# Which tokens open the first pass of a hybrid attention layer

## The chip, the cores and the metric

The kernel runs on one core of one Trainium2 chip. The metric is device time in microseconds (us). The median of three runs before the change is 1921.53 us (1916.76 to 1921.9).

## The reference

One decoder step of a layer that has two groups of heads, for 2048 prompt tokens and for a sample group of 8 x 8 tokens. All data are float32.

```python
xn = rmsnorm(h, g_mix_norm)                      # h: tokens x 1024
z = xn @ w_in
q_c, kv_c, gate_mla, q_g, k_g, v_g, a_g, gate_gla = split(z)   # 256, 160, 512, 256, 256, 512, 16, 512
q = rmsnorm(q_c) @ w_qup                         # 8 heads, 64 + 32 rotary
c_kv, k_rope = rmsnorm(kv_c[:128]), rope(kv_c[128:])
o_mla = attention(q, c_kv, k_rope) * silu(gate_mla)
log_a = log_sigmoid(a_g @ w_gla_a2 + b) / 16
o_gla = rmsnorm(gated_linear_attention(q_g, k_g, v_g, log_a)) * silu(gate_gla)
h = h + concat(o_mla, o_gla) @ w_out
h = h + sigmoid(h @ w_ple_gate) * (p @ w_ple_proj)
y = rmsnorm(h, g_final)
```

Prompt tokens attend causally among themselves; the sample's tokens attend to 4096 cached positions through a page table and to the new ones. The outputs are y, the latents c_kv, the rotary keys and the states of the linear attention, for both groups.

## The kernel before, in words

The program has five stages, of which the change touches the first. Pass A makes, from the first 944 columns of `w_in`, the latents, queries, keys, values, the gates of the attention and the log decays. Pass B is the gated linear attention. Then come the decode attention of the sample interleaved with the prompt's attention, and the output products.

A product of float32 matrices is carried by three float32r passes: each operand is split into hi and lo, and hi x hi, hi x lo and lo x hi are summed in one PSUM bank. `mm3` (L63, L64, L65) does that for 128 or more stationary columns, `mm2` (L71, L72, L74) for the 64 tokens of the sample, where hi and lo stand side by side. A split costs one ScalarE (ACT) or GpSimd (POOL) pass for hi and one VectorE (DVE) pass for lo: L59 and L60 without a scale; with the gain of the norm in `split_scaled`, L134 on ACT or L132 on POOL for hi, and L135 on DVE for lo.

Pass A runs over `macros`, which are groups of tokens: first the sample (64 tokens, one tile), then four prompt macros of 512 tokens, in four tiles of 128 each. The model width of 1024 is cut into 8 blocks of 128 rows.

- `xload` brings x transposed: for the prompt, four DMAs of 512 KB with two blocks each (L170); for the sample, one of 256 KB (L164). For each block ACT squares it (L175), the block is split, and POOL adds the squares up in the tile `acc` (L179), which has one place.
- `load_wide` brings weights in pairs of blocks (L210) or in whole rows (L214) and splits them. `w1` is 432 columns, split by ACT and DVE; `wg`, the gates' 512 columns, and the smaller `wq`, `wk`, `wv` are split by POOL and DVE.
- `scales` makes 1/rms of the tokens from `acc`: matmuls with a vector of ones (L186), DVE (L189), a power on POOL (L190), and then, for the prompt, a diagonal (L196) and a matmul (L197) that spread it along the columns.
- `group1` makes the 432 columns for one tile of tokens in one bank of the PSUM pool `pg`, 24 matmuls over the 8 blocks. `latents` reads that bank: two squares and a copy on ACT (L257 to L259), small operations on POOL (L260 to L263 and L268 to L271), then DVE writes the normalised latents `nat` (L264, L265), which is the last read of the bank. The transposes (L281) and the matmul of the forget gate (L289) follow, in the pool `pt`, which has two banks.
- `gates` makes the 512 gate columns of a prompt macro in four banks, 96 matmuls; `gates_sample` does so for the sample. Then follow `silu`, `forget` (log decays), `queries` and `keys_values`, whose products go to the pool `pq` and are split again (tiles `qq`) and stored to DRAM.

The pool `pg` has 3 banks, `pt` 2, `pq` 3: all eight. Raw loads, split blocks of x and a scratch tile of `forget` share one pool of 12 places of 4 KB in each partition (tile name `x`). An operation that needs a place waits for the last reader of what was there.

The order on each engine's queue is not the order of the code. A planner simulates the program as it is built and writes each engine's list: of what it thinks ready it takes what stands first in the code. On the chip each engine takes its list in that order, and waits where an operand is not there yet. All DMAs of this pass are issued from SyncE (SP).

The code before the loop over macros loads in this order: the sample's x, `w1`, small tables, the x of the first prompt macro, `wg`, then `wq`, `wk`, `wv`. In the loop, the x of the macro after the next one is loaded behind the gates and log decays of the current macro, except in the first round, where it is there already.

Of the kernel before, what the change touches and what calls it, by code (L numbers as in the profile page):

```python
"""One step of a hybrid MLA + GLA decoder layer, prompt group and sample group, on one core.

Products of float32 matrices are carried by float32r passes: each operand is split into
hi + lo (two float32r parts, exact), and hi*hi + hi*lo + lo*hi is accumulated in PSUM.
Small products stay in plain float32.
"""
# [7 lines left out]
F32 = mybir.dt.float32  # L14
F32R = mybir.dt.float32r
# [5 lines left out]
PSUM = bass.MemoryType.PSUM  # L21
DRAM = bass.MemoryType.DRAM

P = 128
D = 1024          # model width
KB = D // P       # 8 blocks of the model width
S = 2048          # prompt tokens
NT = S // P       # 16 prompt tiles
NB, TD = 8, 8     # sample batches, tokens each
SD = NB * TD      # 64 sample tokens  # L30
T = S + SD
PAST = 4096
H, DN, DR, DV = 8, 64, 32, 64
# [8 lines left out]
BASE = 8          # the innermost blocks of the GLA chunk  # L42
FLOOR = -20.0     # least log decay of a step inside them


def emit(ctx, tc, I, O):
# [20 lines left out]
    def mm2(out, a, bh, bl, first, last):  # L67
        """the same for half as many rows: a is [hi | lo], and lo*hi comes out below"""
        m = a.shape[-1] // 2
        if first:  # L70
            T_.matmul(out[:2 * m], a, bh, start=True, stop=False)  # L71
        T_.matmul(out[:m], a[:, :m], bl, start=False, stop=False)  # L72
        if not first:
            T_.matmul(out[:2 * m], a, bh, start=False, stop=last)  # L74
# [20 lines left out]
    # hi and lo parts of queries, keys (both transposed) and values  # L95
# [3 lines left out]
    Kr = dram.tile([DR + 1, 2, S], F32, name="Kr")     # last row: ones  # L99
    Vd = dram.tile([NT, P, H, 2, DV], F32, name="Vd")  # L100
    Ld = dram.tile([2, P, T], F32, name="Ld")          # log decays, [2 heads x 64] by pair, transposed
    Gd = dram.tile([H * DV, T], F32, name="Gd")       # 2 silu(gate), transposed
    Od = dram.tile([H * DV, T], F32, name="Od")       # P v, transposed, not yet divided
    Dd = dram.tile([H, S], F32, name="Dd")            # sums of P
    Rd = dram.tile([H, T], F32, name="Rd")            # their reciprocals
# [11 lines left out]
    # sample group, kept for the decode attention  # L117
# [5 lines left out]

    macros = [(S, SD, [(NT, SD)])]
    macros += [(j * 512, 512, [(4 * j + k, P) for k in range(4)]) for j in range(4)]
# [11 lines left out]
    # ------------------------------------------------------------------ pass A: latents, queries, keys, values  # L137
    def pass_a(wb):
        """returns the weights of pass B, which take the place of this pass's as soon as these are done"""
        with ExitStack() as c:  # L140
# [17 lines left out]
            def xload(t0, W, add):  # L158
                """x^T in two parts, and the sums of squares over each partition's rows"""
# [6 lines left out]
                for k in range(KB):  # L166
# [11 lines left out]
                    if k:  # L178
                        add.tensor_tensor(acc[:, :W], acc[:, :W], sq[:, :W], op=ALU.add)  # L179
                return x, acc  # L180

            def scales(acc, W, tiles):
                """1 / rms of the tokens, along the rows (R) and along the columns"""
# [18 lines left out]
            def load_wide(ws, src, g=None, cp=A):  # L202
                """weights of each 128 rows of src, and of all its columns, into [P, hi|lo, columns] of ws"""
                cols = src.shape[1]
                for k, w in enumerate(ws):
                    if cols <= 512:
# [10 lines left out]
            x, acc = xload(*macros[0][:2], G)  # L217
            load_wide([w[:, :, :432] for w in w1], I["w_in"][:, 0:432], gmix)
# [3 lines left out]
            nc.sync.dma_start(wa2[:17], I["w_a2"])  # L222
            nx = xload(*macros[1][:2], G)
            load_wide(wg, I["w_in"][:, 432:944], gmix, G)
# [25 lines left out]
            def latents(z, q, i, m, lat, la, cs):  # L250
# [33 lines left out]
                # forget gate logits, from the low-rank rows and the row of ones  # L284
# [7 lines left out]
            def forget(la, W, t0):  # L292
                """log sigmoid(x) / 16, with log sigmoid(x) = min(x, 0) - ln(1 + exp(-|x|))"""
# [9 lines left out]
            def gates(x, W, zs, ks):  # L303
                """block of x by block, which lets the next tokens' blocks in one after another"""
# [14 lines left out]
            def gates_sample(x, i, m, t0):  # L319
                """few tokens: they are the stationary side, and the result is transposed"""  # L320
# [59 lines left out]
            for mi, (t0, W, tiles) in enumerate(macros):  # L380
# [4 lines left out]
                nc.sync.dma_start(cs[:, :n], I["cossin"][:, tiles[0][0]:tiles[0][0] + n])  # L385
                rbc = scales(acc, W, tiles)
                for q, (i, m) in enumerate(tiles):
                    z = group1(x, q, m)
                    latents(z, q, i, m, lat, la, cs)
# [20 lines left out]
                else:  # L410
                    # most of the gates last: their operands' places go to the weights of pass B as they are done
# [8 lines left out]
    def weights_b(ww, xp, gm):  # L420
        """in the places of pass A's operands, in the order in which it gives them up"""
# [13 lines left out]
    # ------------------------------------------------------------------ pass B: gated linear attention  # L435
    def pass_b(ws, xp, wb):
        with ExitStack() as c:
# [22 lines left out]
            rst = wp.tile([P, 4, P], F32, name="rst")       # 0 where a cumulation begins, else 1  # L460
# [10 lines left out]
            # second factors [2 heads x 64, pair, head of the pair, token], zero off the diagonal  # L471
# [4 lines left out]
            # state [2 heads x 64, pair, head of the pair, 128], zero off the diagonal  # L476
# [27 lines left out]
            def gla(cnt, i, m, qk, v, gt):  # L504
# [6 lines left out]
                # transposed q, k [2 heads x 64, pair, token] and cumulated log decay  # L511
# [8 lines left out]
                # inside the base blocks a step's log decay is held at -20 (e^-20 is far below a float32's last bit)  # L520
# [23 lines left out]
                # q exp(b), k exp(b_last - b)  # L544
# [13 lines left out]
                # A^T[s, t] by levels: first halves of blocks of 2L against their second halves  # L558
# [59 lines left out]
                # outputs and state  # L618
# [55 lines left out]
                # norm and gate  # L674
# [23 lines left out]
    # ------------------------------------------------------------------ decode attention  # L698
    def decode(c):
        """a generator; each step is a piece of work"""  # L700
# [5 lines left out]
        CK = 8                      # key blocks of 128 in a chunk  # L706
        NCK = 4                     # chunks of a sample
# [15 lines left out]
        # q in the latent space [c, b, hi|lo, h, t], and the rope stack [hi; hi; lo]  # L723
# [12 lines left out]
        qrs = wp.tile([96, NB, 2, H, TD], F32R, name="qrs")    # second half zero: it adds nothing to the lo rows  # L736
# [76 lines left out]
        def fresh(b, mx, dn, oc):  # L813
            """the keys of the new tokens"""
# [74 lines left out]
    # ------------------------------------------------------------------ prompt attention  # L889
    def attention(c, we, slots):  # L890
        """a generator; each step is a block of 128 keys against a tile of 512 queries.
        The places of the keys and values go to slots as they are done."""
# [7 lines left out]
        nc.sync.dma_start(cm, I["cmask"])       # [q, k]: 0 where k <= q, else -1e30  # L900
# [379 lines left out]
```

## Time and profile before

| what | value |
|---|---|
| median of three runs | 1921.53 us (1916.76 to 1921.9) |
| span of the profiled execution | 1922.2 us; no separate time is given for that execution |
| instructions | 27335 |
| TensorE (PE) busy | 1786.5 us |
| VectorE (DVE) busy | 1215.8 us |
| ScalarE (ACT) busy | 919.9 us |
| GpSimd (POOL) busy | 687.2 us |
| mean granted TensorE clock | 0.965 of full speed |
| moved by DMA | 183.74 MB |

The span is the time from the first to the last instruction, and stands 0.7 us above the median of the runs. A row of a view by lines names the line of the kernel, the engine, the operation, the tiles out<-in, their shapes, the count, busy time and mean duration in ns, and the idle time of the engine just ahead with what ended it. A row in order of time gives the start and the duration in us. Matmuls are pipelined, so their pace is read from start to start and not from their durations. PEld is the load of the stationary operand, SPq the queue of SyncE.

### The profile page before, as it was taken

The numbers are of one execution on the slowest core, as the hardware profiler recorded it, in microseconds if no ns is written. First come the engines' busy times: TensorE is split into PE (matmuls) and PEld (weight loads), VectorE is DVE, ScalarE is ACT, GpSimd is POOL, SyncE is SP. The second block draws the span as 40 slices with busy tenths as digits, with TensorE's granted clock in tenths as the row PEclk, the third lists the DMA queues.
The fourth block names the chain that finished last, engine by engine and source line by source line (L and its number), as shares of the span: only waits on it lengthen the run. The fifth ranks groups of instructions, "written<-read, shape, count | busy, mean of one in ns | idle before, by whom it ended". The sixth has DMA issues, their size and how long they took to land.

```text
span 1922.2 us, 27335 instructions
## 1 busy us (share of the span) xinstructions
PE 1786.5 (93%) x9296; PEld 1427.9 (74%) x9296; DVE 1215.8 (63%) x2640; ACT 919.9 (48%) x2184; POOL 687.2 (36%) x1043
## 2 busy tenths in 40 slices
PE   4999987899999996999999999999998999999997
PEld 3877776688787784677777777777776788888885
DVE  6376466566744766788878888888887433323333
ACT  4354455334332433677776777777783112212112
POOL 5263352343433332544444444454436100000000
PEclk7999999899989997899999999999999999999999
DMA  5164476511111107223323232322217432222211
GB/s 167 42 232 158 147 267 212 136 39 38 48 31 45 45 23 178 68 71 94 83 78 100 58 86 72 97 80 77 79 37 237 120 94 83 88 84 73 77 48 33
DMA packets 150374, 183.74 MB, mean 96 GB/s; under 512 B 18682, under 2 KB 93291, under 8 KB 150235
## 3 DMA queue, kind: packets, MB, share of 16 engines
q1 hardware_dynamic: 144090, 161.02, 27.8%
q0 software_dynamic: 6144, 20.98, 3.6%
q8 instruction: 74, 1.21, 0.3%
q14 instruction: 66, 0.53, 0.1%
HBM read 125.60 MB, written 56.35 MB: 95 GB/s over the span
## 4 chain that ended last, share of the span: by engine, by line
PE 67%; DVE 5%; DMA 4%; ACT 2%; issue 1%; POOL 1%; SPq 0%; POOLq 0%; DVEq 0%; ACTq 0%
PE pgE L63 6%; PE pgE L65 6%; PE pgE L64 6%; PE pgB L65 4%; PE pgB L63 4%; PE pgB L64 4%; PE poC L976 3%; PE poC L978 3%; PE psC L963 3%; PE pmC L933 3%; PE poC L977 3%; PE psC L964 3%; PE psC L965 3%; DVE pl L971 1%; PE poD L803 1%
## 5 line engine op out<-in xcount | busy, mean ns | idle before, releaser
L971 DVE TENSOR_TENSOR pl<-pf,ph 128x512 fp32r<-128x512 f32 (+1 forms) x320 | 230.2, 724 | 42.4 <-ACT pf L969 38.2
L967 ACT ACTIVATE ph<-psC 128x512 fp32r<-128x512 f32 (+1 forms) x320 | 171.0, 534 | 126.2 <-PE psC L965 68.6
L969 ACT ACTIVATE pf<-psC 128x512 f32<-128x512 f32 (+1 forms) x320 | 170.2, 532 | 0.0
L935 DVE TENSOR_REDUCE mxC<-pmC 128x1 f32<-128x512 f32 x192 | 129.6, 682 | 30.4 <-PE pmC L933 28.3
L933 PE MATMUL pmC<-KT,qC 96*128 96x512 f32 (+2 forms) x320 | 122.8, 402 | 20.1 <-DVE mxC L940 6.5
L976 PE MATMUL poC<-ph,VT 128*128 128x512 f32 (+1 forms) x320 | 124.0, 387 | 4.5 <-ACT ob L981 3.0
L978 PE MATMUL poC<-pl,VT 128*128 128x512 f32 (+1 forms) x320 | 122.6, 384 | 2.0 <-DVE pl L971 1.8
L963 PE MATMUL psC<-qC,KT 97*128 97x512 f32 (+1 forms) x320 | 121.8, 381 | 0.5 <-ACT pf L969 0.4
L964 PE MATMUL psC<-qC,KT 96*128 96x512 f32 (+1 forms) x320 | 119.0, 372 | 0.0
L965 PE MATMUL psC<-qC,KT 96*128 96x512 f32 (+1 forms) x320 | 118.6, 371 | 0.0
L977 PE MATMUL poC<-ph,VT 128*64 128x512 f32 (+1 forms) x320 | 117.0, 366 | 0.0
L1146 ACT ACTIVATE thE<-pgE 128x512 f32<-128x512 f32 x32 | 19.1, 598 | 153.6 <-PE pgE L65 153.6
L1147 DVE SCALAR_TENSOR_TENSOR thE<-thE,pgE 128x512 f32<-128x512 f32 x32 | 22.0, 688 | 111.0 <-ACT thE L1146 111.0
L933 PEld LDWEIGHTS pmC<-KT,qC 96*128 96x128 f32 x320 | 62.4, 198 | 37.9 <-DVE mxC L935 10.9
L64 PE MATMUL pgE<-wpg,hh 128*128 128x512 f32 x224 | 87.7, 391 | 0.0
L63 PE MATMUL pgE<-wpg,hh 128*128 128x512 f32 x224 | 87.6, 391 | 0.0
L51 POOL TENSOR_SCALAR chl<-cr 128x1024 fp32r<-128x1024 f32 x32 | 38.3, 1198 | 137.4 <-PE poD L803 137.3
L65 PE MATMUL pgE<-wpg,hl 128*128 128x512 f32 x224 | 85.4, 392 | 0.0
L1150 POOL TENSOR_TENSOR ssE<-ssE 128x1 f32<-128x1 f32 (+1 forms) x17 | 3.3, 195 | 219.9 <-ACT yE L1149 219.9
L1090 POOL TENSOR_TENSOR raw<-raw 128x512 f32<-128x512 f32 (+1 forms) x17 | 22.2, 1308 | 161.5 <-DMA raw<-Rd 161.5
L60 DVE TENSOR_TENSOR x<-x 128x512 fp32r<-128x512 f32 (+2 forms) x74 | 64.5, 917 | 22.3 <-PE pgB L64 14.2
L750 POOL DMA_INDIRECT cr<-in_ckv,idx x32 | 36.7, 1148 | 116.5 <-PE poC L978 53.1
(475 smaller groups left out, 5396.3 us busy)
## 6 DMA issues: line engine op xcount, KB each, us to landing
x<-in_xT SPq DMA_DIRECT2D x32, 512.0 KB
x<-in_w_in SPq DMA_DIRECT2D x16, 512.0 KB
Qn<-qq SPq DMA_DIRECT2D x16, 512.0 KB
Kn<-qq SPq DMA_DIRECT2D x16, 512.0 KB
Vd<-qq SPq DMA_DIRECT2D x16, 512.0 KB
KT<-Kn SPq DMA_DIRECT2D x32, 256.0 KB
VT<-Vd SPq DMA_DIRECT2D x8, 1024.0 KB
qC<-Qn SPq DMA_DIRECT2D x32, 256.0 KB
```

Source lines behind the costliest of these rows:

```text
L63: T_.matmul(out, ah, bh, start=first, stop=False)
L64: T_.matmul(out, ah, bl, start=False, stop=False)
L65: T_.matmul(out, al, bh, start=False, stop=last)
L933: T_.matmul(ps[:, :w], qs, kv[0][cb][:96, 0, :w], start=True, stop=True)
L963: T_.matmul(ps[:, c0:], kh[:, ks], qh[:, c0:], start=True, stop=False)
L964: T_.matmul(ps[:, c0:], kh[:96, ks], ql[:, c0:], start=False, stop=False)
L965: T_.matmul(ps[:, c0:], kl[:, ks], qh[:96, c0:], start=False, stop=True)
L967: A.activation(ph[:, c0:], ps[:, c0:], AF.Exp, scale=SC)
L971: V.tensor_tensor(pl[:, c0:], pf[:, c0:], ph[:, c0:].bitcast(F32), op=ALU.subtract)
L976: T_.matmul(o[:, c0:], vt[:, kb, DV:192], ph[:, c0:], start=kb == 0, stop=False)
L977: T_.matmul(o[:DV, c0:], vt[:, kb, 0:DV], ph[:, c0:], start=False, stop=False)
L978: T_.matmul(o[:, c0:], vt[:, kb, DV:192], pl[:, c0:], start=False, stop=kb == nk - 1)
```

## The change

The first prompt macro is moved ahead of the sample: `macros` is now prompt 0, sample, prompt 1, 2, 3. Behind each second block of x that `xload` has split for prompt 0, the matching pair of blocks of `w1` is loaded and split, so that DMAs and splits of x and `w1` alternate. `wg` is then loaded ahead of the x of the second macro, which is now the sample's. For the first macro the products of `group1` go block by block: the outer loop is over the 8 blocks, the inner one over the four tiles, whose sums stand in four banks (three of `pg`, one of `pq`). This loop stands ahead of `scales` in the code. The other macros use `group1` as before. Comments and doc strings are taken out, with the line numbers kept.

```diff
-    macros = [(S, SD, [(NT, SD)])]
-    macros += [(j * 512, 512, [(4 * j + k, P) for k in range(4)]) for j in range(4)]
+    macros = [(j * 512, 512, [(4 * j + k, P) for k in range(4)]) for j in range(4)]
+    macros.insert(1, (S, SD, [(NT, SD)]))
...
-            def xload(t0, W, add):
+            def xload(t0, W, add, beside=None):
...
                     if k:
                         add.tensor_tensor(acc[:, :W], acc[:, :W], sq[:, :W], op=ALU.add)
+                    if beside is not None and k % 2:
+                        beside(k - 1)
                 return x, acc
...
-            def load_wide(ws, src, g=None, cp=A):
+            def load_wide(ws, src, g=None, cp=A, ks=None):
                 cols = src.shape[1]
                 for k, w in enumerate(ws):
+                    if ks is not None and k not in ks:
+                        continue
...
-            x, acc = xload(*macros[0][:2], G)
-            load_wide([w[:, :, :432] for w in w1], I["w_in"][:, 0:432], gmix)
+            def first_weights(k):
+                load_wide([w[:, :, :432] for w in w1], I["w_in"][:, 0:432], gmix, A, (k, k + 1))
+
+            x, acc = xload(*macros[0][:2], G, first_weights)
             gkv = wp.tile([P, CL], F32, name="gkv")
...
+            load_wide(wg, I["w_in"][:, 432:944], gmix, G)
             nx = xload(*macros[1][:2], G)
-            load_wide(wg, I["w_in"][:, 432:944], gmix, G)
...
                 nc.sync.dma_start(cs[:, :n], I["cossin"][:, tiles[0][0]:tiles[0][0] + n])
+                if mi == 0:
+                    zq = [pg.tile([P, 512], F32, name="pg") for q in range(3)] + [pq.tile([P, 512], F32, name="pq")]
+                    for k in range(KB):
+                        for q, z in enumerate(zq):
+                            sl = slice(q * P, q * P + P)
+                            mm3(z[:, :432], x[k][:, 0, sl], x[k][:, 1, sl], w1[k][:, 0, :432], w1[k][:, 1, :432], k == 0, k == KB - 1)
                 rbc = scales(acc, W, tiles)
                 for q, (i, m) in enumerate(tiles):
-                    z = group1(x, q, m)
+                    z = zq[q] if mi == 0 else group1(x, q, m)
                     latents(z, q, i, m, lat, la, cs)
```

## The prediction

> **What bounds the kernel now.** I read the page's busy row first, then a table of pass A by stretches, then the waits and the order of time at its start.
>
> ```profile
> PE 1786.5 (93%) x9296; PEld 1427.9 (74%) x9296; DVE 1215.8 (63%) x2640; ACT 919.9 (48%) x2184; POOL 687.2 (36%) x1043
> ```
>
> TensorE (PE) is busy for 1786.5 of 1922.2 us, so what an edit can win lies in the other 135.7 us and in stretches at half clock. The table has, for each stretch, each engine's busy time, then the granted clock, the DMA share and GB/s.
>
> ```profile
> 0.00:16.50 16.50, 6.84 (x18) 4.24 (x18) 7.54 (x20) 10.63 (x30) 4.15 (x17) 1.00 0.79 250
> 16.50:34.30 17.80, 0.47 (x4) 0.32 (x3) 13.93 (x12) 8.56 (x20) 17.09 (x21) 0.58 0.38 111
> 34.30:40.00 5.70, 5.70 (x17) 4.67 (x17) 4.47 (x13) 0.49 (x2) 3.63 (x5) 0.50 0.32 98
> 40.00:101.00 61.00, 60.72 (x316) 51.17 (x315) 28.16 (x62) 19.29 (x43) 18.76 (x53) 1.00 0.26 78
> 101.00:131.00 30.00, 26.07 (x116) 21.58 (x116) 23.98 (x25) 18.18 (x39) 19.74 (x21) 0.94 0.67 240
> ```
>
> 27 of those idle us lie in the first 34.3. After that PE runs 5.7 us at half clock, 61 us full, and then loses 3.9 us between the first and the second prompt macro (101 to 131). The waits of the first 60 us name one culprit, and the order of time shows it:
>
> ```profile
> PE pt L281 <- DVE nat L264: 17.3, 1, 17.3
> ```
> ```profile
> 29.12 4.69 DVE L264 TENSOR_SCALAR nat<-gt,s 64x256 f32<-64x256 f32 x1 [3.52 <-POOL s L263]
> ...
> 31.64 5.18 POOL L132 TENSOR_SCALAR wg<-x,gmix 128x512 fp32r<-128x512 f32 x4
> ```
> ```profile
> 33.87 0.47 PE L281 MATMUL pt<-ident,nat 64*128 64x64 f32 x2 [17.33 <-DVE nat L264]
> 34.27 0.79 PE L71 MATMUL pg<-wg,x 128*128 128x512 f32 x1
> 34.86 0.56 PE L63 MATMUL pg<-w,x 128*128 128x432 f32 x1
> 35.22 0.56 PE L64 MATMUL pg<-w,x 128*128 128x432 f32 x1
> ```
>
> The sample's transposes (L281) stand ahead of the first prompt products (L63) on PE's queue. They wait 17.3 us for the sample's chain of small operations, which shares POOL and DVE with the splits of x and wg. Meanwhile x and w1 have long been in place. Then spacing is 0.36 us a matmul: half clock.
>
> **The change, part by part.** *Start.* The prompt's x is the first large load, w1 follows pair by pair.
>
> ```profile
> 1.71 0.43 SPq L164 DMA_DIRECT2D x<-in_xT  x1
> ```
> ```profile
> 5.02 0.26 ACT L175 ACTIVATE acc<-x 128x64 f32<-128x64 f32 x1 [2.04 <-DMA x<-in_xT]
> ```
> ```profile
> 6.00:8.00 2.00, 0.00 (x0) 0.00 (x0) 1.06 (x7) 1.28 (x9) 1.21 (x4) 1.00 0.96 315
> ```
>
> The sample's 256 KB took 3.3 us from issue to use; 512 KB takes 0.26 MB / 315 GB/s = 0.8 more: first x pair at 5.9. The w1 pair (442 KB) lands 1.3 later, 7.2. All of x and w1 is 3.9 MB, 12.4 us at 315 GB/s: in by about 17. What a block k (128 rows of the model width) costs each engine:
>
> ```profile
> L179 POOL TENSOR_TENSOR acc<-acc,sq 128x512 f32<-128x512 f32 x7 | 9.7, 1382 | 3.8 <-ACT sq L175 3.6
> L60 DVE TENSOR_TENSOR x<-x 128x512 fp32r<-128x512 f32 x8 | 8.9, 1154 | 1.1 <-ACT x L59 1.1
> L132 POOL TENSOR_SCALAR wg<-x,gmix 128x512 fp32r<-128x512 f32 x8 | 7.9, 1002 | 1.9 <-DMA x<-in_w_in 1.9
> L135 DVE SCALAR_TENSOR_TENSOR wg<-x,gmix,wg 128x512 fp32r<-128x512 f32 x8 | 6.0, 788 | 0.1
> L135 DVE SCALAR_TENSOR_TENSOR w<-x,gmix,w 128x432 fp32r<-128x432 f32 x8 | 5.0, 674 | 2.9 <-ACT w L134 2.8
> L134 ACT ACTIVATE w<-x,gmix 128x432 fp32r<-128x432 f32 x8 | 4.8, 645 | 1.8 <-DMA x<-in_w_in 1.8
> L59 ACT ACTIVATE x<-x 128x512 fp32r<-128x512 f32 x8 | 4.7, 616 | 0.0
> L175 ACT ACTIVATE sq<-x 128x512 f32<-128x512 f32 x7 | 4.3, 620 | 2.5 <-POOL acc L179 2.5
> ```
> ```profile
> 63.00 0.35 PE L65 MATMUL pg<-w,x 128*128 128x432 f32 x1
> 63.20 0.35 PE L63 MATMUL pg<-w,x 128*128 128x432 f32 x1
> ...
> 68.39 0.39 PE L63 MATMUL pg<-x,wg 128*128 128x512 f32 x1
> 68.62 0.39 PE L64 MATMUL pg<-x,wg 128*128 128x512 f32 x1
> ```
>
> ACT 0.62 + 0.62 + 0.65 = 1.9 us, DVE 1.15 + 0.67 = 1.8, POOL 1.4. PE, with all four tiles per block, 12 matmuls every 0.195 us = 2.3 us warm, 4.3 at half clock. So PE paces: with four banks each block that lands feeds 12 matmuls, not 3. ACT's first four passes end at 8.4, w hi at 9.0, w lo at 9.7. Now the first matmul is at 9.7 as well; full speed came 5.1 to 6.5 us after a restart (34.86 to 40.0 by the table; the row below follows the first matmul at 9.66). I take 5.1:
>
> ```profile
> 16.18 0.35 PE L74 MATMUL pg<-w,x 128*128 128x432 f32 x1
> ```
>
> 14 matmuls by 14.8, the other 82 take 16.0: done at 30.8. The upper bound comes from the later macro, where POOL and DVE slow each other more:
>
> ```profile
> L60 DVE TENSOR_TENSOR x<-x 128x512 fp32r<-128x512 f32 x8 | 11.8, 1529 | 0.0
> L179 POOL TENSOR_TENSOR acc<-acc,sq 128x512 f32<-128x512 f32 x7 | 11.3, 1620 | 0.6
> ```
>
> With 1.53 for both DVE passes a block costs 3.06; eight from 6.5 on end at 31, and the last block's matmuls at 33.3. I take 31, near the PE end, since 1.15 and 0.67 are from this very stage.
>
> *After the first products.* The code now asks for the row scales (L186) behind the 96 matmuls, so the chain scales, latents, release of a bank is bare: the 96 hold all three pg banks, and the gates of this macro need them. The same chain in the trace, there hidden under PE work:
>
> ```profile
> 55.26 1.05 PE L186 MATMUL pt<-ones,acc 128*128 128x1 f32 x8
> ...
> 57.85 0.47 ACT L257 ACTIVATE junk<-pg,R 128x256 f32<-128x256 f32 x1 [4.59 <-POOL R L190]
> ...
> 61.42 0.34 DVE L265 SCALAR_TENSOR_TENSOR nat<-pg,s,gkv 128x128 f32<-128x128 f32 x1
> ```
>
> 6.5 us (55.26 to 61.76). I add 1.5 for POOL's queue: the splits of wg and the sample's sums, whose tile acc has one place and comes free only with L186. So gates start at 39.0 (bounds: 33 if L186 slips in early; 45, rival below). After 7 us idle PE again runs some 5.7 us at half clock and loses 2.9.
>
> *Sum of the start.* In us of work at full clock: before, at 40.0, PE has done the sample's first products (16 x 0.195 = 3.1) and half of 5.7 (2.9): 6.0. After, at 44.7, it has done 96 x 0.195 = 18.7 and 2.9: 21.6, where the kernel before would be at 40.0 + 15.6 = 55.6. Gain 10.9.
>
> *The sample second.* Its PE work is the same, but now fills the gap at 101 to 131: its first products and gates are 3.1 + 16 x 0.23 = 6.8 us that need no x of the next macro, beside the queries and keys that stand there already. There 3.9 us idle and, by the clock 0.94 over 30 us, 1.8 us of lost speed are to be had: up to 5.7; its chain could also add waits, as it did at 17 us: at worst minus 4, one macro gap (3.9) once more. I take 3, since POOL and DVE are 80% and 66% busy there and take the sample's operations on top.
>
> *Moved loads.* wg goes ahead of the sample's x (4 DMAs of 512 KB ahead of one of 256 KB); its POOL splits (8 x 1.0) and DVE splits (8 x 0.8) fit between 20 and 31. If that cover goes, they stand before the gates: up to 8. SP's count of DMAs is unchanged; with x's 8 blocks held, 4 of the 12 places turn over, so the fourth x pair waits at SP until the first is split (about 9), and w1's last pair and wg queue behind; PE needs that block at 26. The next prompt's xload comes behind the sample's gates and log decays; its eight DVE passes (11.8 us) lie beside 6.8 us of the sample's and 60 x 0.23 = 13.8 us of the queries', keys' and values' matmuls. The removed comments cost nothing.
>
> The rest is shifted. Span 1922.2 - 10.9 - 3 = 1908.3; the page gives no separate time for the profiled execution, its span is 0.7 above the median of the runs, so **1907.6**.
>
> **The rivals.**
> *B, scales early.* If L186 is put into the stretch of the 96, R is ready when they end, and the first bank is free after 61.76 - 57.85 = 3.9 us less the 1.8 (9 matmuls) by which tile 0 ends first: 2 us of gap and no fall of the clock. Gates at 33, gain 10.9 + 6 + 2.9 + 3 = 23: 1899. For it: the sums of squares are there by about 20, so L186 has 11 us in which it could run. Against: the code asks for it behind the 96, and they are ready too. The Trainium skill (TensorE: Matmul & The Clock Gate, section on what is actually happening) halves the clock after an idle window of about 3.4 us, which would spare a gap of 2; the trace agrees for the long one, 0.50 after 17 us.
>
> *C, POOL is late.* The queue order was fixed by a planner that put L281 17 us too early; POOL's sums and splits (7 x 1.62, 8 x 1.0) may stand ahead of R. These two rows show a sum and an x split, each alone:
>
> ```profile
> 27.59 1.25 POOL L179 TENSOR_TENSOR acc<-acc,sq 128x512 f32<-128x512 f32 x1
> ```
> ```profile
> 15.88 0.69 DVE L60 TENSOR_TENSOR x<-x 128x512 fp32r<-128x512 f32 x1 [0.76 <-ACT x L59]
> ```
>
> If they start at 7 and nothing of POOL overlaps DVE's two-input passes, 7 x (1.25 + 0.69 + 0.67) and 8 x (1.00 + 0.79) end near 40, R's power near 41, and a bank is free at 45: 6 us less than forecast, and with no gain at the second gap 1917. That strict exclusion is what the Trainium skill says (SBUF — State Buffer, section on who interferes with whom). For it: 1.53 and 1.62 when both run. Against: by strict exclusion they would be 1.25 + 0.69 = 1.94, so overlap is partial.
>
> *D, slower.* The sample's transposes stand between gates and later prompt products; the wait of 17.3 us comes back there, since its L264 again reads SBUF beside POOL's x sums. 1922 - 10.9 + 4 (POOL) + 17.3 = 1932. It decides from a wait of 11 us on.
>
> **How the numbers follow.** A measurement here can tell about 0.3%, 5.8 us. Forecast 0.50 (1902 to 1914), B 0.18, C 0.22, D 0.10. Faster: 0.50 + 0.18 + 0.07 (a third of C) = 0.75; same: the other 0.15 of C; slower: D, 0.10. The range, 1896 to 1919, reaches over B and C and leaves D out and some of each end.
>
> **What would show it.** Right: first L63 near 9.7, 96 of them dense to about 31; an idle of 6 to 9 us there, ended by L264 or L265; half clock behind it; less than 3.9 us idle before the second prompt macro; the macros after it as long as now. Wrong: L186 among the 96 (B), POOL without a gap from 7 to 38 (C), a PE wait of over 11 us on L264 behind 60 us (D), or pass B and attention taking another time than before, as a new plan might.

## The result, and the profile after

The changed kernel is slower: 1931.88 us median (1925.44 to 1938.86, 20 runs) against 1919.78 us for the kernel before in the same series (1913.49 to 1929.82, 20 runs), a ratio of 1.0062 with an interval of [1.0048, 1.0076]. That is 12 us more, where 13.9 us less was forecast. The profiled execution has a span of 1931.6 us. In the changed file the lines of pass A that the prediction names stand lower: `scales` L186 to L197 are now L188 to L199, the latents' L263 to L265 are L269 to L271, their transposes L281 are L287, forget's L296 is L302, the gate's store L317 is L323.

The page's busy row: PE has about as much to do as before (1793.1 against 1786.5 us).

```profile
PE 1793.1 (93%) x9296; PEld 1433.8 (74%) x9296; DVE 1213.0 (63%) x2640; ACT 921.7 (48%) x2184; POOL 694.2 (36%) x1043
```

The waits of PE in the first 120 us. A row gives the total in us, the number of waits and the longest one. The wait of 17.3 us on the sample's `nat` is gone. The first row, for the first weights, the kernel before has in its way too (9.7 us, at the sample's L71). The others add up to 22.5 us, where the kernel before has 2.7 in this stretch beside the two long waits.

```profile
PE pg L63 <- ACT w L134: 9.2, 1, 9.2
PE pt L199 <- DVE diag L198: 9.0, 4, 7.0
PE pq L63 <- DVE qq L60: 6.7, 9, 1.6
PE pt L287 <- issue: 4.8, 1, 4.8
PE pg L63 <- ACT x L59: 2.0, 1, 2.0
```

The table by stretches (same columns as in the prediction's first table) shows where they lie.

```profile
0.00:9.20 9.20, 0.00 (x0) 0.00 (x0) 2.27 (x5) 4.48 (x8) 1.78 (x9) 1.00 0.66 189
9.20:30.50 21.30, 21.29 (x104) 20.32 (x104) 18.67 (x18) 10.37 (x19) 13.08 (x11) 1.00 0.80 249
30.50:48.30 17.80, 3.97 (x14) 2.80 (x13) 9.91 (x23) 6.03 (x29) 15.14 (x30) 0.57 0.28 78
48.30:76.20 27.90, 27.90 (x122) 22.22 (x121) 10.25 (x21) 7.07 (x18) 6.38 (x27) 0.91 0.15 46
76.20:117.20 41.00, 32.25 (x148) 23.36 (x146) 22.83 (x54) 20.81 (x37) 12.44 (x21) 0.93 0.65 229
117.20:135.00 17.80, 17.17 (x80) 16.28 (x80) 12.14 (x9) 7.73 (x14) 11.00 (x8) 0.87 0.27 103
135.00:175.00 40.00, 36.94 (x164) 30.48 (x165) 12.68 (x28) 12.34 (x33) 10.46 (x41) 0.91 0.10 29
```

The same stage in the kernel before, from the end of the first prompt macro's gates to the end of the second's:

```profile
93.00:102.50 9.50, 8.42 (x37) 6.01 (x35) 7.29 (x12) 6.16 (x9) 3.77 (x4) 1.00 0.50 168
102.50:132.00 29.50, 26.36 (x120) 22.09 (x121) 23.91 (x28) 17.10 (x38) 19.16 (x24) 0.94 0.71 257
132.00:165.10 33.10, 33.10 (x158) 27.07 (x159) 12.81 (x26) 10.99 (x26) 6.57 (x28) 1.00 0.34 115
```

Two things are to be seen. First, the 96 products run without a gap from 9.2 to 30.5, as forecast, but behind them PE does 4 us of work in 17.8, and POOL is busy 15.14 of these. Second, from 76.2 to 117.2 PE idles 8.8 us: 6.7 of these are nine waits of products of the keys, the values and the sample's queries on DVE's splits (`qq`, L60), with no other product ready to fill them, and 2.0 is the wait for the second macro's x. The kernel before has 1.1 us idle between the gates of its first prompt macro and the second one's first product. Then the second macro's own chain of scales, which before lay under keys and values, is bare too, that is, without other work of PE to hide it: 135 to 175 has 3.1 us idle and a clock of 0.91, where the kernel before has 33.1 of 33.1 at full clock.

In order of time, the first hole (start and duration in us, all engines, rows chosen along the chain):

```profile
30.25 0.28 PE L188 MATMUL pt<-ones,acc 128*128 128x1 f32 x2
...
30.98 4.03 DVE L135 SCALAR_TENSOR_TENSOR wg<-x,gmix,wg 128x512 fp32r<-128x512 f32 x4 [2.04 <-POOL wg L132]
...
35.61 0.15 DVE L191 TENSOR_SCALAR R<-pt 128x4 f32<-128x4 f32 x1
...
35.84 1.22 POOL L192 TENSOR_TENSOR R<-R,mhalf 128x4 f32<-128x4 f32 x1 [2.03 <-DVE R L191]
...
39.68 0.91 POOL L132 TENSOR_SCALAR wq<-x,gq 128x768 fp32r<-128x768 f32 x1
40.63 1.02 DVE L135 SCALAR_TENSOR_TENSOR wq<-x,gq,wq 128x768 fp32r<-128x768 f32 x1 [0.84 <-POOL wq L132]
40.68 1.02 POOL L267 TENSOR_SCALAR s<-s 128x1 f32<-128x1 f32 x1
...
42.81 0.19 POOL L267 TENSOR_SCALAR s<-s 128x1 f32<-128x1 f32 x1
...
46.11 0.80 POOL L269 TENSOR_SCALAR s<-s,R 128x2 f32<-128x2 f32 x1
...
47.35 0.34 DVE L271 SCALAR_TENSOR_TENSOR nat<-pg,s,gkv 128x128 f32<-128x128 f32 x1
...
48.27 0.78 PE L63 MATMUL pg<-x,wg 128*128 128x512 f32 x1
```

DVE takes four splits of `wg` and then the sample's x ahead of the first step of `R`, which so starts 5.1 us after its operand's last matmul (30.25 + 0.28). POOL has splits of `wg` to do until 33.8 and then waits 2.03 us for that step. From 37 on POOL is the bound: the four little steps of the first latents (L266 to L269) stand there between the splits of `wq` and `wk`, five sums of the sample's x, and the second tile's steps. Three of the four are longer too, where a DVE split runs beside them. L267 takes 1.02 us beside the split of `wq` at 40.63 and ends with it; the second tile's takes 0.19 (42.81). In the kernel before the first tile's L260, L261 and L263 took 0.19, 0.19 and 0.27 us; here the same steps (L266, L267, L269) take 0.97, 1.02 and 0.80. From `R` to the end of L271 the first tile takes 47.69 - 37.06 = 10.6 us; in the kernel before the same steps took 3.9 (57.85 to 61.76). The gates start at 48.27, where 39.0 was forecast.

The second hole is made on SP's queue. The changed kernel:

```profile
105.99 4.21 SPq L384 DMA_DIRECT2D Vd<-qq  x3
110.34 0.66 SPq L341 DMA_DIRECT2D Gd<-th  x1
111.05 0.58 SPq L170 DMA_DIRECT2D x<-in_xT  x1
```

The kernel before:

```profile
94.92 1.09 SPq L317 DMA_DIRECT2D Gd<-gt  x2
96.54 0.90 SPq L170 DMA_DIRECT2D x<-in_xT  x2
```

In the loop a round asks for the x of the macro that comes next (`macros[mi + 1]`), not of the one after that. So in the kernel before the second prompt macro's x is issued right behind the first one's gates (at 96.5), and the queries and keys cover its loading and splitting. In the changed one it is asked for in the sample's round and stands behind three stores of `Vd` and the sample's gate store, which waits for the sample's transposes. It goes at 111.05. The last product of the values starts at 106.58, so only small products of the sample's queries are left to cover it, and the products of the second macro are not there to fill the waits on `qq`.

### The profile page after: what moved, and what is told of

Read it like the earlier page. It is cut to its first block, busy times and chain, and to the rows that moved or that the text cites. A ratio compares the mean times of both kernels' runs of the same rounds, so it can differ in the third digit from the quotient of the medians.

```text
span 1931.6 us, 27315 instructions
## 1 busy us (share of the span) xinstructions
PE 1793.1 (93%) x9296; PEld 1433.8 (74%) x9296; DVE 1213.0 (63%) x2640; ACT 921.7 (48%) x2184; POOL 694.2 (36%) x1043
## 4 chain that ended last, share of the span: by engine, by line
PE 65%; DVE 5%; DMA 4%; ACT 2%; issue 2%; POOL 1%; SPq 0%; POOLq 0%; ACTq 0%; DVEq 0%
PE pgE L63 7%; PE pgE L65 7%; PE pgE L64 6%; PE pgB L65 4%; PE pgB L63 4%; PE pgB L64 4%; PE pmC L945 3%; PE poC L988 3%; PE poC L990 3%; PE psC L975 3%; PE psC L977 3%; PE psC L976 3%; PE poC L989 2%; DVE pl L983 1%; PE poD L815 1%
## 5 line engine op out<-in xcount | busy, mean ns | idle before, releaser
L63 PE MATMUL pgE<-wpg,hh 128*128 128x512 f32 x224 | 87.9, 392 | 0.0
L60 DVE TENSOR_TENSOR x<-x 128x512 fp32r<-128x512 f32 (+2 forms) x74 | 69.4, 981 | 28.1 <-PE pgB L64 15.0
L776 POOL TENSOR_TENSOR chl<-cr,chl 128x1024 fp32r<-128x1024 f32 x32 | 76.7, 2396 | 1.3
```

The source lines that it names most:

```text
L63: T_.matmul(out, ah, bh, start=first, stop=False)
```

## The experiments

All are edits of the changed kernel unless said otherwise; ratios are to the kernel before in the same series. The theories: T1, the second macro's x is issued too late. T2, the sample's own chain costs waits between prompt macros, wherever its x stands. T3, the bare chain from the 96 products to the gates costs the time, in the form a (its length reaches the end of the kernel) or b (something behind it waits anyway). T4, added later: the order on POOL sets that chain's length.

**x_early.** While the first prompt macro runs, the x of the third entry of `macros` is asked for already.

```diff
-                acc = s1.tile([P, 512], F32, name="acc")
+                acc = s1.tile([P, 512], F32, name="acc", bufs=2)
...
-                    x, acc = nx if mi == 0 else xload(*macros[mi + 1][:2], G)
+                    if mi == 0:
+                        x, acc = nx
+                        nx = xload(*macros[2][:2], G)
+                    elif mi == 1:
+                        x, acc = nx
+                    else:
+                        x, acc = xload(*macros[mi + 1][:2], G)
```

> The changed kernel with one edit: the x of the second prompt macro is asked for in round 0, behind the log decays of prompt 0 and ahead of its queries, instead of behind the sample's gates and log decays (the tile acc gets a second place for it). Theory T1 (x comes late: in the changed kernel its first DMA left at 111.05 us, 35 us after the gates of prompt 0 had ended): the first of these DMAs now leaves near 78 us, the first products of the second prompt macro lie beside the queries, keys, values and the sample, and 12 to 20 us come back: ratio to the kernel before 0.995 to 1.000. Theory T2 (the sample's own chain in mid-pass costs, whatever x does): less than 5 us come back, ratio 1.003 to 1.006. Theory T3 (the loss is in the first 50 us): no difference, 1.006.

Measured: 1921.28 us, ratio 1.0017 [0.9998, 1.0037]. Its SP queue, in order of time:

```profile
71.25 0.38 SPq L323 DMA_DIRECT2D Gd<-gt  x1
71.68 0.45 SPq L170 DMA_DIRECT2D x<-in_xT  x1
```

The x leaves 39 us earlier, beside the gates' stores, and the first product of the second macro starts at 89.20 and not at 117.2. Some 9 of the 12 us are back. T1 holds in its direction; the 12 to 20 us that it had expected were too many.

**acc2.** The control for x_early: only the second place of `acc`, the load where the changed kernel has it.

> The changed kernel with one difference: two places for the sums of squares, tile acc, as x_early had it, but the load of the second prompt macro stays where it is asked for, behind the sample's log decays. It separates the two halves of x_early. T1 (the place in the order of the load matters): as the changed kernel, ratio to before 1.005 to 1.007, the load leaves at 108 to 112 us. Rival T1b (the one place of acc was the trouble): as x_early, 1.000 to 1.003.

Measured: 1930.48 us, ratio 1.0067 [1.0048, 1.0086]; the x leaves at 109.11. It is the place of the load that x_early gained by, not the place for the sums.

**scales_first.** `rbc = scales(acc, W, tiles)` stands ahead of the loop of the 96 products.

```diff
+                rbc = scales(acc, W, tiles)
                 if mi == 0:
                     zq = [pg.tile([P, 512], F32, name="pg") for q in range(3)] + [pq.tile([P, 512], F32, name="pq")]
...
-                rbc = scales(acc, W, tiles)
```

> The changed kernel with one edit: the row scales of the first macro are asked for ahead of its 96 products in the code, not behind them. In the changed kernel PE is idle or on small work from 30.5 to 48.3 us. Theory T3a (the chain of the scales is bare because it is asked for late, and its DVE step then stands behind four wg splits): R is ready before the products end, the gates start at 38 to 41 us instead of 48.3, 7 to 11 us come back, ratio 1.000 to 1.003. Rival T3b (POOL's and DVE's other work, the sample's sums and wq, sets the end of that chain anyway): gates at 45 or later, less than 4 us come back, ratio 1.004 to 1.006.

Measured: 1927.23 us, ratio 1.0049 [1.0034, 1.0064]. `R`'s power is now at 30.28 and the gates start at 40.61, 7.7 us earlier, but the time comes only 2.5 us nearer to the kernel before by the ratios and 4.4 by the medians, and the interval overlaps that of the changed kernel. The x of the second macro still leaves only at 108.59: the earlier gates ran into the second hole. As a prediction of the size T3a fails here.

**x_early_scales.** Both edits together.

> x_early and scales_first together: the second prompt macro's x is asked for in the first prompt macro (with a second place for acc), and the row scales are asked for ahead of the first 96 products. Theory T1 (the loss is the late x of the second prompt macro, which also swallowed the gain of earlier gates): with x early, the 7.7 us by which scales_first moved the gates now reach the end, 5 to 8 us less than x_early: ratio to before 0.997 to 0.999, gates of the first macro near 40. Rival T3b (the gates' start is not on the path, something behind it waits anyway): no change against x_early, ratio 1.001 to 1.003.

Measured: 1916.17 us against 1916.15 for the kernel before, ratio 0.9995 [0.9981, 1.0009]; gates at 40.34. Against x_early the gates start 5.9 us earlier (46.21 to 40.34). That is worth some 4 us by the ratios (1.0017 to 0.9995), though the two intervals overlap, and 7.3 at `Gd 2` in the table of milestones below. The interval ends just below T3b's 1.001 to 1.003 and holds only the upper half of T1's 0.997 to 0.999: the milestones say that the gates' start counts once x is early; the times alone do not settle it.

**tiles.** The block-by-block loop is taken out, so that the first macro's products go tile by tile by `group1` as in all others; the alternating loads stay.

> The changed kernel without the four banks: the first macro's products go tile by tile, as in all other macros; order of macros and alternating loads stay. Theory T3a: tile 0 ends when its last block is there (near 25 us), its latents then run beside tiles 1 to 3, whose products end near 40; the gates follow without a gap and at full clock: 5 to 11 us come back, ratio 1.000 to 1.004. Rival (block by block is what feeds PE at the start): PE idles between 9 and 25 us, the products end at 45 or later, the time is that of the changed kernel or longer, ratio 1.006 to 1.010.

Measured: 1932.98 us, ratio 1.0080 [1.0052, 1.0109]. PE is busy for only 17.04 us between 9 and 30, where the changed kernel is without a gap, and the gates start at 47.89, no earlier. What holds the gates up is not the same, though:

```profile
27.62 1.48 POOL L192 TENSOR_TENSOR R<-R,mhalf 128x4 f32<-128x4 f32 x1
```
```profile
40.98 0.71 PE L63 MATMUL pg<-w,x 128*128 128x432 f32 x1
```

`R`'s power stands 8.2 us earlier on POOL than in the changed kernel, and the first bank is free at 40.4, 7.3 us earlier. But three banks hold three tiles, so the fourth tile's products have waited for that bank and start only at 40.98. The gates follow them. What the earlier chain won, these products cost: the intervals of the two kernels overlap.

**no_alt.** The loads of x and `w1` do not alternate.

```diff
-            x, acc = xload(*macros[0][:2], G, first_weights)
+            x, acc = xload(*macros[0][:2], G)
+            load_wide([w[:, :, :432] for w in w1], I["w_in"][:, 0:432], gmix)
```

> The changed kernel without the alternation: all of x of the first macro is loaded and split, then w1; order of macros and four banks stay. If alternation matters as the change means it: w1's first pair lands only after 2 MB of x, first product at 13 to 17 us instead of 9.2, and PE then paces, so the products end 3 to 6 us later than 30.5 and the time grows by as much: ratio 1.007 to 1.010. Rival (the bare chain behind the products is what counts and it hides the later start): the gates start where they did, within 2 us of 48.3, ratio 1.005 to 1.007.

Measured: 1939.29 us, ratio 1.0113 [1.0086, 1.0141], 7 us more than the changed kernel by the medians, 10 by the ratios. Two products of the trace:

```profile
18.61 1.45 PE L63 MATMUL pg<-w,x 128*128 128x432 f32 x3 [18.61 <-ACT w L134]
```
```profile
99.43 0.79 PE L63 MATMUL pq<-lat,wq 128*128 128x512 f32 x1 [6.92 <-DVE qq L60]
```

The first product is at 18.6 and not at 9.2, and the last of the 96 starts at 42.18 and not at 30.05. So alternating the loads feeds PE sooner, as it was meant to. But the gates start at 49.27, only 1.0 us later than in the changed kernel, as the rival had it (its ratio of 1.005 to 1.007 was too low): the splits and the chain behind the products hid the later start. The lost time shows further on, in one wait of 6.9 us among the queries and in the second macro's x, which leaves at 118.04. What the alternation itself is worth this run does not show.

**sample_third.** x_early_scales with the sample behind the second prompt macro: `macros.insert(2, ...)`; the second macro's x is loaded behind the first one's gates, and the sample's and the third prompt macro's in the second.

> x_early_scales with the sample moved on by one macro: order prompt, prompt, sample, prompt, prompt. The second prompt macro's x is loaded behind the first one's gates, beside its queries and keys; the sample's x is loaded in the second macro, and the third prompt macro's x there too. The sample's splits and sums are thereby out of POOL's and DVE's way in the gap before the first gates. T1 and T4 (that gap is set by POOL and DVE taking the sample's operations between the steps of the first latents): gates of the first macro at 36 to 39, ratio 0.993 to 0.998. Rival T2 (the sample among the prompt macros costs its own waits wherever it stands): the loss is the same as in x_early_scales, within 2 us.

Measured: 1918.09 us, ratio 1.0010 [0.9993, 1.0026]. Within the interval it is x_early_scales, as T2 said for this run and against what T1 and T4 expected. It does not show the sample's place alone, since the gates start at 44.07, 3.7 us later than there: with the sample's operations gone, the splits of `wq`, `wk` and `wv` have moved up on POOL between the steps of the latents. So it was not the sample alone that stood in the way.

**xe_sc_late.** x_early_scales, with the sample's x, `wq`, `wk` and `wv` asked for behind the first macro's latents.

```diff
-            nx = xload(*macros[1][:2], G)
...
-            load_wide(wq, I["w_qup"], gq, G)
...
-            load_wide([wk], I["w_uk"], cp=G)
...
-            load_wide([wv], I["w_uv"], cp=G)
...
                     latents(z, q, i, m, lat, la, cs)
+                if mi == 0:
+                    nx = xload(*macros[1][:2], G)
+                    load_wide(wq, I["w_qup"], gq, G)
+                    load_wide([wk], I["w_uk"], cp=G)
+                    load_wide([wv], I["w_uv"], cp=G)
```

> x_early_scales, with the load of the sample's x and of the weights wq, wk and wv asked for behind the first macro's latents, not ahead of its products. On POOL the first latents' steps then come some places earlier among the splits, on SP nothing moves. T4 (POOL's order sets the gap before the first gates): gates 1 to 3 us earlier than in x_early_scales, ratio 0.001 to 0.002 lower. Rival: the planner's order is almost the same, no difference above 1 us.

Measured: 1911.99 us, ratio 0.9980 [0.9965, 0.9995]: faster than both kernels. The order in which POOL takes the latents' steps is now such (in order of time):

```profile
29.77 1.47 POOL L192 TENSOR_TENSOR R<-R,mhalf 128x4 f32<-128x4 f32 x1
31.24 1.36 POOL L132 TENSOR_SCALAR wg<-x,gmix 128x512 fp32r<-128x512 f32 x2
32.68 0.50 POOL L262 TENSOR_SCALAR s<-s 128x1 f32<-128x1 f32 x1
...
35.92 0.26 POOL L265 TENSOR_SCALAR s<-s,R 128x2 f32<-128x2 f32 x1
36.16 0.90 POOL L132 TENSOR_SCALAR wq<-x,gq 128x768 fp32r<-128x768 f32 x1
```

L262 to L265 are the steps that the changed kernel has as L266 to L269. Its first latent needs no split of `wq`, and the gates start at 37.33, 3.0 us earlier than in x_early_scales and 10.9 earlier than in the changed kernel. T4 holds for the gates; the ratio is 0.0015 lower than that of x_early_scales, with intervals that overlap.

**xe_sc_late2.** The same kernel again.

> The version xe_sc_late once more, to narrow its interval and to see how much the profile of one program differs between two executions. If the gain of 0.2% is real: ratio to before 0.996 to 0.999, first store of MGd near 388 us again. If it was chance: 0.999 to 1.001. The stretch from the first store of Od to the end took 1088 to 1098 us in the profiles of versions that do the same there; if that is spread between executions, this version's 1097.7 becomes another number of that span.

Measured: 1912.42 us against 1920.11, ratio 0.9966 [0.9948, 0.9984]. The gain stands; span of the profiled execution 1908.2. Some of its stretches:

```profile
30.00:37.40 7.40, 3.18 (x13) 2.06 (x12) 6.41 (x19) 4.30 (x24) 7.06 (x13) 0.69 0.37 111
...
65.00:100.00 35.00, 31.96 (x142) 26.84 (x141) 28.87 (x34) 20.57 (x38) 19.92 (x22) 0.90 0.51 168
100.00:125.00 25.00, 23.00 (x108) 19.62 (x107) 12.87 (x40) 11.59 (x30) 9.68 (x29) 0.80 0.71 247
125.00:156.00 31.00, 31.00 (x150) 25.15 (x149) 10.55 (x22) 9.24 (x19) 4.06 (x20) 1.00 0.11 32
```

**xe_sc_act.** xe_sc_late with the high parts of `wq`, `wk` and `wv` written by ScalarE: `load_wide(wq, I["w_qup"], gq)` and so on.

> xe_sc_late with the high parts of wq, wk and wv written by ScalarE and not by POOL: four operations of 0.6 to 0.9 us leave POOL's queue between the steps of the first latents. T4 (POOL's queue sets the gap between the 96 products and the gates): the sample's gap shrinks, gates of the first macro at 36 to 37 and the second to fourth latents 2 to 3 us earlier, ratio 0.0005 to 0.0015 lower than xe_sc_late2. Rival T4b (the rest of the gap is R's power, which stands behind six splits of wg, and DVE): no difference above 1 us.

Measured: 1912.97 us, ratio 0.9959 [0.9941, 0.9978]; gates at 37.05. Against xe_sc_late2 it is 0.0007 by the ratios, with intervals five times as wide: no difference that can be told. The second latents are done 4.9 us earlier than there (L267 ends at 40.53 and not at 45.42) and the third 2.4, but the gates' start moves by only 0.4: the first latents were free of these splits already.

**before_again, after_again.** Both kernels unaltered, one profile more of each.

> The kernel before, unaltered, for a second profile. If the plan alone sets the times of pass A, the third prompt macro's start and the first store of MGd come within 1 us of the first profile (395.3). If from the first store of Od to the end it takes 1088 to 1098 us (1096.3 in the first profile), that stretch varies between executions, and differences there are no effect of the change.

> The changed kernel, unaltered, for a second profile. If the loss is made in pass A by its order, the first store of MGd again comes 15 to 18 us later than before's (412.2 in the first profile), and first Od to the end again takes 1088 to 1098 us (1091.6).

Measured: spans of 1915.6 and 1921.9, against 1922.2 and 1931.6 in the first profiles. The kernel before repeats pass A within 0.2 us (first `MGd` at 395.26 and 395.30) and then differs by 6.4 us from the first `Od` on. The changed kernel is already 3.5 us apart at `Gd 2` and 6.1 at `MGd` (406.11 and 412.23), which comes 10.8 us later than in the kernel before and not 15 to 18, against the expectation. So the profiled execution that this text reads shows more loss in pass A than another one, and the sizes below are those of this one execution.

The milestones of the profiled executions, in us from the span's start: first gate product of the first prompt macro, first issue of the second prompt macro's x, last store of the second prompt macro's gates (`Gd`), first store of `MGd` (pass B), first store of `Od`, and from there to the end. For the kernel before the first column is left out, since there the sample comes ahead of these gates; for sample_third the third is, since there the sample comes behind them.

| kernel | gates | x issued | Gd 2 | MGd | Od | rest | ratio |
|---|---|---|---|---|---|---|---|
| before | | 96.54 | 165.08 | 395.30 | 825.89 | 1096.3 | 1 |
| before_again | | 96.31 | 164.88 | 395.26 | 825.66 | 1089.9 | |
| after | 48.27 | 111.05 | 175.67 | 412.23 | 840.00 | 1091.6 | 1.0062 |
| after_again | 47.12 | 108.55 | 172.16 | 406.11 | 832.52 | 1089.4 | |
| no_alt | 49.27 | 118.04 | 180.76 | 415.58 | 846.34 | 1096.4 | 1.0113 |
| tiles | 47.89 | 105.84 | 170.64 | 405.81 | 836.23 | 1095.9 | 1.0080 |
| acc2 | 47.48 | 109.11 | 174.32 | 409.37 | 837.67 | 1092.5 | 1.0067 |
| scales_first | 40.61 | 108.59 | 172.60 | 407.75 | 838.69 | 1089.2 | 1.0049 |
| x_early | 46.21 | 71.68 | 167.65 | 403.72 | 827.86 | 1088.8 | 1.0017 |
| sample_third | 44.07 | 68.86 | | 392.21 | 823.13 | 1091.0 | 1.0010 |
| x_early_scales | 40.34 | 70.73 | 160.32 | 392.10 | 822.26 | 1087.7 | 0.9995 |
| xe_sc_late | 37.33 | 68.68 | 158.21 | 387.68 | 816.67 | 1097.7 | 0.9980 |
| xe_sc_late2 | 37.44 | 68.70 | 156.66 | 387.08 | 815.20 | 1093.0 | 0.9966 |
| xe_sc_act | 37.05 | 67.83 | 155.52 | 385.54 | 817.08 | 1090.0 | 0.9959 |

The ratios follow the columns `Gd 2` to `Od` in the main; tiles is the exception, with a higher ratio than its milestones would give. The column `rest` varies by 10 us with no order in it, and by 4.7 and 6.4 us between two executions of one program (1097.7 and 1093.0; 1096.3 and 1089.9): no effect of an edit can be told there.

## Why the prediction was wrong

The sign was wrong, and two terms of the sum did it. At the milestone `Gd 2` the forecast of 13.9 us less had turned into 10.6 more (7.1 in the second profile): 24.5 us to explain.

**The start, up to the 96 products: right.** First L63 at 9.21 (forecast 9.7), dense to 30.5 (forecast 31). Four banks and alternating loads make PE start early and run dense, as no_alt (first product at 18.6) and tiles (17.04 us busy between 9 and 30) show from the other side; what that is worth in time, neither shows. That the end came out so close is in part luck: the products are 0.36 us apart only until 12.26, so full speed was back 3.3 us after the first one and not 5.1 (the table's clock of 1.00 for this stretch does not show that slow start), while six of the eight matmuls for the scales, L188, were put in among the 96 at 25.67 and took 0.6 us. The prediction had named that as a sign of rival B. The last two stand behind the products, at 30.25, so `R` could not come sooner.

**The term "6.5 us, and 1.5 for POOL's queue": mis-sized.** It came out at 17.8 us, and the gates at 48.27, not 39.0. Rival C named the engine and gave 45, but its reason was another: it had POOL fall behind in its sums (they ended at 21.7, well before the last matmuls of L188 read them). Its case rested on how much POOL and DVE hold each other up. The argument against it, that 1.53 and 1.62 are less than 1.94, does not hold, since the splits' mean mixes those with a sum beside them and those without. In the kernel before two splits of x with sums beside them take 3.47 us (at 106.65) and three sums 5.03 (at 107.95), so a pair takes some 1.7 us, where a split and a sum alone took 0.69 and 1.25. That is nearly one after the other. In fact the chain's small steps were spread over two queues, behind the splits of `wg` and the sample's x on DVE, among those of `wq`, `wk` and the sample's sums on POOL. The 6.5 us had been measured where these queues were almost free. The prediction had said what it costs "if that cover goes": up to 8 us more; it was 9.3. By its own formula, with gates at 48.3, the gain at the start is 10.9 - 9.3 = 1.6 us. With the scales asked for early and the queue put right (xe_sc_late2) the gap is 7.4 us, and the gates start at 37.4. That this lies near the forecast of 8.0 is luck, since a part of the chain then runs under the products; in xe_sc_late the first tile still takes 5.7 us from `R` (31.24) to the end of L267 (36.96), not 3.9.

**The term "the sample second", plus 3 us: wrong in sign.** From the first gates' end to `Gd 2` the changed kernel has 8.8 + 0.6 + 3.1 = 12.4 us idle and, by the clocks 0.93, 0.87 and 0.91 of the three stretches, 2.3 + 2.2 + 3.3 = 7.8 of lost speed (PE's busy time, times what the clock falls short of 1). The kernel before has 1.1 + 3.1 + 0 = 4.2 idle and 26.36 x 0.06 = 1.6 of lost speed. That is 14.4 us worse instead of 3 better. The step that failed is the sentence that the next prompt's `xload` "comes behind the sample's gates and log decays" and its DVE passes "lie beside" the sample's and the queries' matmuls. The first half was right, and it excludes the second: what stands behind the sample's last steps is issued when that covering work is over (the sample's first products and gates ended at 91, the last product of the values began at 106.58, the x left at 111.05). And without products of the second macro beside them, the keys, the values and the sample's queries waited 6.7 us for DVE's splits. The lower bound, minus 4, was taken from one macro gap and was too near. The two terms make 9.3 + 17.4 = 26.7 of the 24.5 us; the working by mean clocks is no better than that.

**"The rest is shifted": off by some us.** From `Gd 2` to `MGd` the kernel before takes 230.2 us and the changed one 236.6, 234.0 in the second profile. The third prompt macro takes part of it: from `Gd 2` to the last store of its own gates it is 68.1 us before and 70.6 and 70.3 after. Another part shows in the waits of PE behind that, before and after (at L623 and L635 of pass B):

```profile
PE poB L623 <- POOL qe L547: 7.2, 1, 7.2
```
```profile
PE poB L635 <- POOL qe L559: 10.7, 1, 10.7
```

In the second profiles these waits are 7.4 and 10.3 us. Why the planner's order costs more there has not been settled. From `MGd` to `Od` it is 430.6 before against 427.8 and 426.4: a little comes back.

**The rivals.** D had the right sign with a wrong mechanism: no wait of over 11 us on the sample's `nat` shows up in mid-pass, and that its 1932 is the measured time is luck. B's edit, scales early, was tried (scales_first) and did not give 1899: the row scales ran early, but the chain's later steps stayed among the splits on POOL's queue (gates at 40.61, where B had 33), and then the late x took the gain.

**What of the forecast gain is real.** With both faults repaired (xe_sc_late2, xe_sc_act) the new order is worth 6.5 to 8 us by the ratios, 8 to 11 at `Gd 2` and `Od`, of the 13.9 forecast. By the prediction's own formula the start is all there: with gates at 37.4 its term becomes 10.9 + 1.6 = 12.5. The sample second is still no gain: from 65 to 156 xe_sc_late2 has 3.0 + 2.0 us idle and 3.2 + 4.6 of lost speed (clocks 0.90 and 0.80), 12.8 in all, where the kernel before loses 5.8 between its two macros. That leaves 12.5 - 7 = 5.5 against 8.4 measured at `Gd 2`, which is as near as mean clocks come.

A bare chain costs clock as well. Behind the 17.8 us with little work the first gates start 0.43 us apart (48.85 to 49.28), where full speed is 0.23. The Trainium skill (TensorE: Matmul & The Clock Gate, section on what is actually happening) has the clock halved after an idle window; the trace agrees here. Behind the short holes of the second macro's scales, none over 1.7 us by itself, it fell too:

```profile
133.45 0.95 PE L188 MATMUL pt<-ones,acc 128*128 128x1 f32 x8
136.09 0.49 PE L199 MATMUL pt<-diag,ones 128*128 128x128 f32 x2 [1.69 <-DVE diag L198]
136.96 0.49 PE L199 MATMUL pt<-diag,ones 128*128 128x128 f32 x2 [0.38 <-DVE diag L198]
137.82 0.49 PE L199 MATMUL pt<-diag,ones 128*128 128x128 f32 x2 [0.38 <-DVE diag L198]
139.53 0.87 PE L287 MATMUL pt<-ident,nat 128*128 128x128 f32 x3 [1.22 <-DVE nat L270]
140.05 0.71 PE L63 MATMUL pg<-w,x 128*128 128x432 f32 x1
140.56 0.56 PE L64 MATMUL pg<-w,x 128*128 128x432 f32 x1
140.92 0.56 PE L65 MATMUL pg<-w,x 128*128 128x432 f32 x1
```

From 140.56 on products start every 0.36 us, not every 0.195. So a bare chain costs twice: its holes, and half speed behind them.

## What to carry to other kernels

When a macro is put between two others, follow the load of the one after it: ask at which row of the DMA queue it is issued now, and which matmuls are left from that moment on; cover that is done before the load leaves covers nothing. A chain of small operations is not costed by the sum of its steps in a quiet stage, but by the queues that it has to pass in the new one: list what stands between its steps on each engine. A gain at the start may be swallowed by the next hole, so that one repair alone looks worthless (scales_first: gates 7.7 us earlier, 2.5 to 4.4 us at the end, not clear of the noise); try the two together before giving either up.

## What the runs showed that was not expected

Several short holes of 0.4 to 1.7 us with small matmuls between them brought the clock down as one long idle did (0.36 us spacing from 140.56 on). The kernel before has a case too: behind waits of 0.28, 0.80 and 1.40 us (98.64 to 105.34) its products start 0.36 us apart from 106.58 to 108.02. The Trainium skill (TensorE: Matmul & The Clock Gate, section on what is actually happening) names an idle window of about 3.4 us. None of these holes is that long by itself.

Small POOL steps took as long as the DVE split beside them (1.02 us and not 0.19), so the price of a step depends on what the other engine does meanwhile.

The same program's profiles differ by 6.1 us in the changed kernel up to `MGd` (406.11 and 412.23) and by 6.4 us in the kernel before from the first `Od` on, so a single profile's span cannot tell edits of this size apart. The milestones of one stage do better where they repeat, as in the kernel before (165.08 and 164.88 at `Gd 2`), but not in the changed one (175.67 and 172.16).
